# One pair in two of the second MLP product by seven block products, with two of their weight sums made by adding DMAs

## The chip, the cores and the metric

The kernel runs on one core of a Trainium2 chip. The metric is the time of one execution on the device, in microseconds (us). Engines and queues are named as the profile names them: PE (TensorE, matmuls), PEld (its weight loads), DVE (VectorE), ACT (ScalarE), POOL (GpSimd) and SP, whose queue issues the DMAs of the kernel before.

## What is computed

One layer of a bidirectional encoder on 256 tokens of width 2048, in float32: mixed attention, cross attention to 256 memory tokens, and an MLP of width 8192, each followed by a layer norm. The change touches the last of them:

```python
def squared_relu_mlp(h, w_mlp_in, w_mlp_out):
    return jnp.square(jax.nn.relu(h @ w_mlp_in)) @ w_mlp_out

ff = squared_relu_mlp(x, w_mlp_in[l], w_mlp_out[l])
x = layer_norm(ALPHA * x + ff, ln3_g[l], ln3_b[l])
```

## The kernel before

**Precision.** A float32 factor is split into a high part hi (a copy by ACT into the fast matmul type, L80) and a rest lo (a subtraction by DVE, L81). `mm3` (L145 to L148) multiplies two split factors by three matmuls: high by high, high by low, low by high. Four buffers for weights' hi and four for lo (`w_hi`, `w_lo`, 1024 columns each) pass the weights to TensorE.

**Stages of the MLP.** The 8192 hidden rows are worked off in four chunks (c) of 16 tiles of 128. In each chunk come four *hidden groups* (g) of four tiles: `hidden_group` multiplies the normed tokens `x2t` by eight double steps of `w_mi` (loaded 1 MB at a time into three buffers `raw`) and `hidden` squares the result (L726 to L728) and splits it into `ht`. Then come two *pair products* (q = 0 and 1, each 1024 output columns; the last chunk has q = 0 only and finishes with plain products from `w_ml`). So there are seven pair products.

**A pair product.** `pair_product(c, q)` takes the chunk's 16 row tiles of `w_mo` as eight pairs (p). A pair's unit is 1 MB: four blocks of 512 columns, in the order b12, b11, b22, b21. With the four blocks of `ht` it is a two by two block product. A *plain* pair takes eight block products of three matmuls, 24 matmuls of 512 columns, from two splits of 1024 columns. A pair listed in `SEVEN` takes seven block products, 21 matmuls, after Winograd's scheme; it needs four sums of weight blocks. `hidden` makes the sums of activations for such a pair (four small subtractions and additions, L743, and a split into `sums_h`) once per chunk. In the kernel before `SEVEN` holds pairs 2, 5 and 7. Their weight sums are made by DVE (L789): one instruction of 1024 columns (b11 + b12 and b22 + b12, with b12 broadcast) and two of 512 (the former's half + b22, and that + b21, each on the sum before it). Such a pair is split in four parts, of 1024, 512, 1024 and 1024 columns.

**Ends of a product.** Four results in `acc` are added to the residual rows `res` by DVE (L846 or L849, here called first adds), four in `att` are copied out by ACT (L857) and eight adds of 512 columns (L852) are left in a list `side`. `part` makes one split and then pops one weight sum from the list `sums`, or, if there is none, one piece of `side`.

**Loads.** `load_unit` issues the load of a unit two pairs ahead from SP. Units 0, 1, 4 and 5 use two fixed halves of a big tile `wx`, the others the three `raw` buffers. The other half of `wx` holds the two buffers of weight sums, used in turn. `wx` takes the place of the first half of hidden group 0's weights (`wide_0`), so nothing may be written there before TensorE has read these. During the hidden groups 1 and 2 of chunk 0 the residual's gain and bias rows (`ln2_g`, `ln2_b`, 256 KB each, broadcast to all partitions) come through `tmp` buffers, and DVE applies them (L566).

**Order.** A scheduler places each engine's instructions by its own estimate of the time; each engine then works them off strictly in that order, and each queue issues its DMAs in order.

Of the kernel before, what the change touches and what calls it, by code (L numbers as in the profile page):

```python
# [12 lines left out]
F32R = mybir.dt.float32r  # L13
BF16 = mybir.dt.bfloat16
AF = mybir.ActivationFunctionType
ALU = mybir.AluOpType
# [22 lines left out]
def encoder_kernel(ctx: ExitStack, tc: tile.TileContext, t, out):  # L39
# [672 lines left out]

    early.close()
    late = ctx.enter_context(tc.tile_pool(name="late", bufs=1))
    SEVEN = ((2, 5, 7), (2, 5, 7))
    s_in = Stream(t["w_mi"][4:])
    sts = [stats_tile() for _ in range(NB)]
    ht = big3("ht")
    sums_h = late.tile([P, 3072], F32R, name="sums_h").rearrange("p (u l c) -> p u l c", l=2, c=512)
    wx = big.tile([P, 8192], F32, tag="big", name="wx")  # L720
    raw2, sums_w = [[wx[:, o:o + 2048] for o in (i, i + 2048)] for i in (0, 4096)]

# [36 lines left out]
    def hidden_group(nexts, tiles, j0):  # L759
# [7 lines left out]
        for i in range(0, G, 2):  # L767
# [1 line left out]

    units = [(c, q, p) for c in range(NCH) for q in range(2) for p in range(CH // 2)  # L770
             if not (c == NCH - 1 and q == 1)]
    loaded, sums, slots = deque(), deque(), [0]

    def load_unit(chunk):

        if not units or units[0][0] != chunk:
            return
        c, q, p = units.pop(0)
        seven = p in SEVEN[q]
        raw = raw2[p % 4] if p % 4 < 2 else raw_tile()  # L780
        nc.sync.dma_start(raw, t["w_mo"][(c * 2 + q) * (CH // 2) + p])
        s = None
        if seven:
            s = sums_w[slots[0] % 2]
            slots[0] += 1
            b12, b22, b21 = [raw[:, o:o + 512] for o in (0, 1024, 1536)]

            def add(out, a, b):
                sums.append(lambda: nc.vector.tensor_tensor(out=out, in0=a, in1=b, op=ALU.add))  # L789
            add(s[:, 0:1024].rearrange("p (i c) -> p i c", i=2), raw[:, 512:1536].rearrange("p (i c) -> p i c", i=2),  # L790
                b12[:, None, :].broadcast_to([P, 2, 512]))
            add(s[:, 1024:1536], s[:, 0:512], b22)
            add(s[:, 1536:2048], s[:, 1024:1536], b21)
        loaded.append((raw, s))

    def part(src):
        w = src.shape[1]
# [9 lines left out]
    def pair_product(c, q):  # L807

        x11, x12, x21, x22 = [acc_tile() for _ in range(4)]
        p1, p5, p6, p7 = [att_tile() for _ in range(4)]  # L810
        plain = [p for p in range(CH // 2) if p not in SEVEN[q]]
        for p in range(CH // 2):
            load_unit(c)
            raw, s = loaded.popleft()
            k = 2 * p

            def a(k_, b):
                return ht[:, k_, b * P:(b + 1) * P], ht[:, k_, S + b * P:S + (b + 1) * P]

            def sm(i):  # L820
                u = SEVEN[0].index(p)
                return sums_h[:, u, 0, i * P:(i + 1) * P], sums_h[:, u, 1, i * P:(i + 1) * P]

            if p in SEVEN[q]:
                first, last = p == SEVEN[q][0], p == SEVEN[q][-1]
                while sums:
                    sums.popleft()()
                for src, todo in ((raw[:, 512:1536], ((p1, a(k, 0), first), (x12, sm(3), False))),
                                  (raw[:, 1536:2048], ((x11, a(k + 1, 0), False),)),
                                  (s[:, 0:1024], ((p5, sm(0), first), (p7, sm(2), first))),  # L830
                                  (s[:, 1024:2048], ((p6, sm(1), first), (x21, a(k + 1, 1), False)))):
                    for (hi, lo), (ps, (ah, al), start) in zip(part(src), todo):
                        mm3(ps, ah, al, hi, lo, start, last)
            else:
                for i in range(2):
                    w = part(raw[:, i * 1024:(i + 1) * 1024])
                    for (hi, lo), to in zip(w, ((x12, x22), (x11, x21))):
                        for b in range(2):
                            ah, al = a(k + i, b)
                            mm3(to[b], ah, al, hi, lo, p == 0 and i == 0, to[b] is x22 and p == plain[-1] and i == 1)  # L840
        cols = [slice((2 * q + i) * 512, (2 * q + i + 1) * 512) for i in range(2)]
        r11, r12, r21, r22 = [res[b][:, cc] for b in range(NB) for cc in cols]

        def first_add(r, ps):
            if c == 0:
                nc.vector.scalar_tensor_tensor(out=r, in0=r, scalar=ALPHA, in1=ps,  # L846
                                               op0=ALU.mult, op1=ALU.add)
            else:
                nc.vector.tensor_tensor(out=r, in0=r, in1=ps, op=ALU.add)  # L849

        def add(o, x, y, op=ALU.add):
            side.append(lambda: nc.vector.tensor_tensor(out=o, in0=x, in1=y, op=op))  # L852

        first_add(r22, x22)
        m1, m5, m7, m6 = [tmp_tile() for _ in range(4)]
        for m, ps in ((m1, p1), (m5, p5), (m7, p7), (m6, p6)):
            nc.scalar.activation(m, ps, AF.Copy)  # L857
        first_add(r12, x12)
        first_add(r11, x11)
        first_add(r21, x21)  # L860
        add(r22, r22, m5)
        add(r12, r12, m5)
        add(m6, m1, m6)
        add(m7, m6, m7)
        add(r11, r11, m1)
        add(r12, r12, m6, ALU.subtract)
        add(r21, r21, m7)
        add(r22, r22, m7, ALU.subtract)
        if c == NCH - 1:
            for b, r in ((0, r11), (0, r12), (1, r21), (1, r22)):  # L870
                side.append(lambda b=b, r=r: stats(sts[b], r))

    for c in range(NCH):
        for g in range(CH // G):
            first = c == 0 and g == 0
            if g == CH // G - 1:
                load_unit(c)
                load_unit(c)
            hidden_group((lambda k: w_mi0[k // 2]) if first else (lambda k: s_in.next()),
                         att_tile if g % 2 else acc_tile, g * G)  # L880
            if first:
                side.extend(residual("ln2"))
        for q in range(2):
            if c < NCH - 1 or q == 0:
                pair_product(c, q)
                continue
            s_ml = Stream(t["w_ml"])
            for n in (2, 3):
                if n == 3:
                    pump(len(side))  # L890
                    wide_w = [big.tile([P, 8192], F32R, tag="big", name=f"w{i}") for i in range(2)] + [None]
                    ps = proj_tokens(None, ht, CH, 512, by_block=True, wide=last_weights, tiles=att_tile)
                else:
                    ps = proj_tokens(s_ml, ht, CH, 512, by_block=False, tiles=acc_tile)
                for b, o, w, p_ in ps:
                    r = res[b][:, n * 512 + o:n * 512 + o + w]
                    nc.vector.tensor_tensor(out=r, in0=r, in1=p_[:, :w], op=ALU.add)
                    stats(sts[b], r)
# [139 lines left out]
```

## Time and profile before

| | |
|---|---|
| runs of the kernel before | 1108.9, 1110.0, 1110.2 us (median 1110.02) |
| profiled execution | 1109.3 us, of it 1107.5 us span |
| granted TensorE clock, mean | 0.996 |
| chunk 0: hidden groups 0 to 3 | about 402 to 493 us |
| chunk 0: products q = 0, q = 1 | 492.9 to 534.4, 534.4 to 575.9 us |
| bytes moved, mean | 215.86 MB, 195 GB/s |

A row of a timeline gives its start, its length, engine, line, operation, output and inputs with their shapes, how many instructions are merged and, in square brackets, how long the engine had been idle before and what ended this. A row of windows gives, for one stretch of time, the busy time of each engine with its count of instructions, the granted clock, the mean busy share of the sixteen DMA engines, and the rate. Successive instructions of one engine overlap by some 0.09 us in DVE's rows, so the step from start to start is shorter than one row's length. Starts are in microseconds from the start of the span.

### The profile page before, as it was taken

To read this page: it belongs to the slowest core of one execution; us is meant where nothing else is said; L and a number is where in the kernel's file an instruction comes from. 1 tells how busy PE (TensorE), PEld (TensorE's weight loads), DVE (VectorE), ACT (ScalarE), POOL (GpSimd) and SP (SyncE) were. 2 spreads that over 40 slices of the span, in tenths; PEclk is the share of its full clock that TensorE was granted. 3 is DMA by queue.
4 is the path that set the end of the run, shared out by engine and by line. 5 is a ranking of instruction groups with operands and counts; after the bars stand their busy time and mean duration, and the time that the engine had idled before them with its cause. 6 is when DMAs were issued, how large, how long until landed. Compare 5 with 4: busy or idle time off the path is not lost.

```text
span 1107.5 us, 15288 instructions
## 1 busy us (share of the span) xinstructions
PE 1091.5 (99%) x5941; PEld 942.8 (85%) x5941; DVE 858.3 (77%) x1257; ACT 587.2 (53%) x860; POOL 38.3 (3%) x45
## 2 busy tenths in 40 slices
PE   9999999999999999999999999999999999999996
PEld 6988899988999878888888888888888888888885
DVE  6878677688879687888977678978678887677796
ACT  6555566545576444455555445555445555555550
POOL 1402000000100000000000000000000000000000
PEclk9999999999999999999999999999999999999998
DMA  9664453466567427744566555455544556555372
GB/s 332 232 229 141 154 195 128 173 220 246 180 205 271 146 78 267 256 165 184 191 225 214 186 183 214 178 206 190 197 184 171 209 197 224 188 190 191 114 260 82
DMA packets 37944, 215.86 MB, mean 195 GB/s; under 512 B 4336, under 2 KB 5232, under 8 KB 14192
## 3 DMA queue, kind: packets, MB, share of 16 engines
q1 hardware_dynamic: 37872, 214.89, 54.4%
q8 instruction: 46, 0.75, 0.3%
q14 instruction: 26, 0.21, 0.1%
HBM read 212.78 MB, written 2.10 MB: 194 GB/s over the span
## 4 chain that ended last, share of the span: by engine, by line
PE 96%; DMA 2%; DVE 1%; SPq 0%; ACT 0%; issue 0%; POOL 0%; DVEq 0%; ACTq 0%
PE acc L147 15%; PE acc L146 15%; PE acc L148 15%; PE acc L195 11%; PE att L195 11%; PE att L200 5%; PE acc L200 5%; PE att L148 3%; PE att L147 3%; PE att L146 3%; PE acc L188 2%; PE acc L186 2%; PE acc L187 2%; PE att L535 1%; PE att L350 1%; DMA raw<-in_w_ka 1%
## 5 line engine op out<-in xcount | busy, mean ns | idle before, releaser
L81 DVE TENSOR_TENSOR w_lo<-raw,w_hi 128x1024 fp32r<-128x1024 f32 (+2 forms) x318 | 365.3, 1162 | 129.6 <-ACT w_hi L80 127.3
L80 ACT ACTIVATE w_hi<-raw 128x1024 fp32r<-128x1024 f32 (+2 forms) x318 | 318.0, 1011 | 275.6 <-PE acc L148 103.0
L80 ACT ACTIVATE w_hi<-wx 128x1024 fp32r<-128x1024 f32 x98 | 100.8, 1031 | 119.5 <-PE acc L148 85.5
L81 DVE TENSOR_TENSOR w_lo<-wx,w_hi 128x1024 fp32r<-128x1024 f32 x98 | 115.0, 1185 | 53.9 <-ACT w_hi L80 53.9
L195 PE MATMUL att<-x2t,w_hi 128*128 128x512 f32 x512 | 139.6, 394 | 0.0
L147 PE MATMUL acc<-w_lo,ht 128*128 128x512 f32 x354 | 137.8, 389 | 0.0
L148 PE MATMUL acc<-w_hi,ht 128*128 128x512 f32 x354 | 137.7, 389 | 0.0
L195 PE MATMUL acc<-x2t,w_hi 128*128 128x512 f32 x480 | 132.3, 394 | 0.0
L146 PE MATMUL acc<-w_hi,ht 128*128 128x512 f32 x354 | 111.4, 389 | 0.0
L195 PEld LDWEIGHTS att<-x2t,w_hi 128*128 128x128 f32 x512 | 88.1, 189 | 12.3
L195 PEld LDWEIGHTS acc<-x2t,w_hi 128*128 128x128 f32 x480 | 82.6, 189 | 11.5
L200 PEld LDWEIGHTS att<-x2t,w_lo 128*128 128x128 f32 x512 | 77.5, 189 | 10.2
L200 PEld LDWEIGHTS acc<-x2t,w_lo 128*128 128x128 f32 x480 | 73.3, 189 | 9.5
L200 PE MATMUL att<-x2t,w_lo 128*128 128x256 f32 x512 | 80.2, 281 | 0.0
L147 PEld LDWEIGHTS acc<-w_lo,ht 128*128 128x128 f32 x354 | 66.5, 188 | 14.0 <-DVE w_lo L81 0.2
L146 PEld LDWEIGHTS acc<-w_hi,ht 128*128 128x128 f32 x354 | 66.4, 188 | 13.8
L148 PEld LDWEIGHTS acc<-w_hi,ht 128*128 128x128 f32 x354 | 66.4, 188 | 13.8
L200 PE MATMUL acc<-x2t,w_lo 128*128 128x256 f32 x480 | 77.0, 281 | 0.0
L147 PE MATMUL acc<-w_lo,xt 128*128 128x512 f32 (+2 forms) x192 | 69.4, 363 | 0.6 <-DVE w_lo L81 0.6
L148 PE MATMUL acc<-w_hi,xt 128*128 128x512 f32 (+2 forms) x192 | 69.1, 361 | 0.0
L146 PE MATMUL acc<-w_hi,xt 128*128 128x512 f32 (+2 forms) x192 | 65.6, 361 | 1.0 <-ACT w_hi L80 1.0
L148 PE MATMUL acc<-w_hi,ot 128*128 128x512 f32 (+1 forms) x136 | 51.9, 382 | 0.0
(244 smaller groups left out, 1876.7 us busy)
## 6 DMA issues: line engine op xcount, KB each, us to landing
raw<-in_w_mi SPq DMA_DIRECT2D x64, 1024.0 KB, 4.9
wx<-in_w_mo SPq DMA_DIRECT2D x28, 1024.0 KB, 4.8
raw<-in_w_mo SPq DMA_DIRECT2D x28, 1024.0 KB, 4.8
raw<-in_w_out SPq DMA_DIRECT2D x16, 1024.0 KB, 4.9
raw<-in_w_ml SPq DMA_DIRECT2D x8, 1024.0 KB, 5.0
raw<-in_w_b SPq DMA_DIRECT2D x5, 1024.0 KB, 4.8
raw<-in_w_qa SPq DMA_DIRECT2D x16, 256.0 KB, 5.4
raw<-in_w_qa SPq DMA_DIRECT2D x4, 1024.0 KB, 4.9
```

Source lines behind the costliest of these rows:

```text
L80: pin(nc.scalar.activation(hi, src, AF.Copy), pinned)
L81: return pin(nc.vector.tensor_tensor(out=lo, in0=src, in1=f(hi), op=ALU.subtract), pinned)
L146: nc.tensor.matmul(ps, ah, bh, start=start, stop=False)
L147: nc.tensor.matmul(ps, ah, bl, start=False, stop=False)
L148: nc.tensor.matmul(ps, al, bh, start=False, stop=stop)
L186: nc.tensor.matmul(ps, hi, xt[:, k, 0:S], start=k == 0, stop=False)
L187: nc.tensor.matmul(ps, hi, xt[:, k, S:2 * S], start=False, stop=False)
L188: nc.tensor.matmul(ps, lo, xt[:, k, 0:S], start=False, stop=k == nk - 1)
L195: nc.tensor.matmul(ps, hi[:, i * P:(i + 1) * P], xt[:, k, :], start=k == 0, stop=k == nk - 1)
L200: nc.tensor.matmul(ps[:, 0:S], lo[:, i * P:(i + 1) * P], xt[:, k, 0:S], start=False, stop=False)
L350: nc.tensor.transpose(pp[:, st * S + b * P:st * S + b * P + P], ev[:, b, st * P:(st + 1) * P], ident)
L535: nc.tensor.transpose(ps[:, o:o + P], x(b, k // 4)[:, (k % 4 + j) * P:(k % 4 + j + 1) * P], ident)
```

## The change

`SEVEN` becomes pairs 1, 3, 5 and 7, in both q. Of the four weight sums of such a pair two are now made in memory: `load_halves` has SP load block b12 twice, side by side, into a buffer of 1024 columns, and then has POOL issue a DMA that adds the blocks b11 and b22 (1024 columns) onto it. Three such buffers stand in the former sums' place and are refilled in turn: the first three in chunk 0 ahead of hidden groups 1 to 3, each later one when a pair has been used. DVE makes the other two sums (512 columns each) in a single buffer `t24`. A unit of such a pair is loaded without its first 512 columns.

```diff
-    SEVEN = ((2, 5, 7), (2, 5, 7))
+    SEVEN = ((1, 3, 5, 7), (1, 3, 5, 7))
...
-    sums_h = late.tile([P, 3072], F32R, name="sums_h").rearrange("p (u l c) -> p u l c", l=2, c=512)
+    sums_h = late.tile([P, 4096], F32R, name="sums_h").rearrange("p (u l c) -> p u l c", l=2, c=512)
...
-    loaded, sums, slots = deque(), deque(), [0]
+    loaded, sums, halves = deque(), deque(), deque()
+    sevens = deque(u for u in units if u[2] in SEVEN[u[1]])
+    t24 = sums_w[0][:, 0:1024]
+    spare = deque([sums_w[0][:, 1024:2048], sums_w[1][:, 0:1024], sums_w[1][:, 1024:2048]])
+
+    def load_halves():
+
+        if not sevens:
+            return
+        c, q, p = sevens.popleft()
+        s, src = spare[0], t["w_mo"][(c * 2 + q) * (CH // 2) + p]
+        spare.rotate(-1)
+        nc.sync.dma_start(s.rearrange("p (i c) -> p i c", i=2),
+                          src[:, 0:512][:, None, :].broadcast_to([P, 2, 512]))
+        nc.gpsimd.dma_start(s, src[:, 512:1536], accum_op=ALU.add)
+        halves.append(s)
...
-        nc.sync.dma_start(raw, t["w_mo"][(c * 2 + q) * (CH // 2) + p])
-        s = None
+        o = 512 if seven else 0
+        nc.sync.dma_start(raw[:, o:], t["w_mo"][(c * 2 + q) * (CH // 2) + p][:, o:])
+        s, todo = None, []
         if seven:
-            s = sums_w[slots[0] % 2]
-            slots[0] += 1
-            b12, b22, b21 = [raw[:, o:o + 512] for o in (0, 1024, 1536)]
-
-            def add(out, a, b):
-                sums.append(lambda: nc.vector.tensor_tensor(out=out, in0=a, in1=b, op=ALU.add))
-            add(s[:, 0:1024].rearrange("p (i c) -> p i c", i=2), raw[:, 512:1536].rearrange("p (i c) -> p i c", i=2),
-                b12[:, None, :].broadcast_to([P, 2, 512]))
-            add(s[:, 1024:1536], s[:, 0:512], b22)
-            add(s[:, 1536:2048], s[:, 1024:1536], b21)
-        loaded.append((raw, s))
+            s = halves.popleft(), t24
+            b22, b21 = raw[:, 1024:1536], raw[:, 1536:2048]
+            for o, a, b in ((t24[:, 0:512], s[0][:, 0:512], b22), (t24[:, 512:1024], t24[:, 0:512], b21)):
+                todo.append(lambda o=o, a=a, b=b: nc.vector.tensor_tensor(out=o, in0=a, in1=b, op=ALU.add))
+        loaded.append((raw, s, todo))
...
-            raw, s = loaded.popleft()
+            raw, s, _ = loaded.popleft()
+            if loaded:
+                sums.extend(loaded[0][2])
...
-                                  (s[:, 0:1024], ((p5, sm(0), first), (p7, sm(2), first))),
-                                  (s[:, 1024:2048], ((p6, sm(1), first), (x21, a(k + 1, 1), False)))):
+                                  (s[0], ((p5, sm(0), first), (p7, sm(2), first))),
+                                  (s[1], ((p6, sm(1), first), (x21, a(k + 1, 1), False)))):
...
+                load_halves()
...
+            if c == 0 and 0 < g:
+                load_halves()
```

In the changed kernel the lines behind these move: the weight sums of DVE are L803 (before: L789), the first adds L859 and L862 (L846 and L849), the epilogue's adds L865 (L852), the broadcast loads L784, the adding DMAs L786 and the unit loads L797 (L781).

**The turn from q = 0 to q = 1 in chunk 0, on DVE.** In the program before these rows stand behind the last split of q = 0. `w_lo_5363` and `w_lo_5380` belong to pair 0, `w_lo_5399` and `w_lo_5416` to pair 1, which is plain.

```order
L846 SCALAR_TENSOR_TENSOR res0_1487<-res0_1487,acc_5041 128x512
L846 SCALAR_TENSOR_TENSOR res0_1487<-res0_1487,acc_5040 128x512
L81 TENSOR_TENSOR w_lo_5363<-wx_4240,w_hi_5362 128x1024
L81 TENSOR_TENSOR w_lo_5380<-wx_4240,w_hi_5379 128x1024
L852 TENSOR_TENSOR res0_1487<-res0_1487,tmp_5341 128x512
L852 TENSOR_TENSOR res1_1488<-res1_1488,tmp_5342 128x512
L852 TENSOR_TENSOR res0_1487<-res0_1487,tmp_5342 128x512
L846 SCALAR_TENSOR_TENSOR res1_1488<-res1_1488,acc_5042 128x512
L81 TENSOR_TENSOR w_lo_5399<-wx_4240,w_hi_5398 128x1024
L852 TENSOR_TENSOR tmp_5344<-tmp_5341,tmp_5344 128x512
L81 TENSOR_TENSOR w_lo_5416<-wx_4240,w_hi_5415 128x1024
L852 TENSOR_TENSOR tmp_5343<-tmp_5344,tmp_5343 128x512
```

In the changed program the same place reads as follows; `w_lo_5424` is the first part of pair 1, which is now one of seven products.

```order
L859 SCALAR_TENSOR_TENSOR res0_1487<-res0_1487,acc_5054 128x512
L859 SCALAR_TENSOR_TENSOR res0_1487<-res0_1487,acc_5053 128x512
L803 TENSOR_TENSOR wx_4240<-wx_4240 128x512
L81 TENSOR_TENSOR w_lo_5388<-wx_4240,w_hi_5387 128x1024
L81 TENSOR_TENSOR w_lo_5405<-wx_4240,w_hi_5404 128x1024
L865 TENSOR_TENSOR res0_1487<-res0_1487,tmp_5366 128x512
L865 TENSOR_TENSOR res1_1488<-res1_1488,tmp_5367 128x512
L865 TENSOR_TENSOR res0_1487<-res0_1487,tmp_5367 128x512
L803 TENSOR_TENSOR wx_4240<-wx_4240 128x512
L859 SCALAR_TENSOR_TENSOR res1_1488<-res1_1488,acc_5055 128x512
L81 TENSOR_TENSOR w_lo_5424<-wx_4240,w_hi_5423 128x1024
L865 TENSOR_TENSOR tmp_5369<-tmp_5366,tmp_5369 128x512
```

Directly behind it, still on DVE in the changed program, come pair 1's other three parts (`w_lo_5435`, `w_lo_5443`, `w_lo_5454`) and the first part of pair 2 (`w_lo_5468`):

```order
L81 TENSOR_TENSOR w_lo_5435<-wx_4240,w_hi_5434 128x512
L865 TENSOR_TENSOR tmp_5368<-tmp_5369,tmp_5368 128x512
L865 TENSOR_TENSOR res0_1487<-res0_1487,tmp_5369 128x512
L81 TENSOR_TENSOR w_lo_5443<-wx_4240,w_hi_5442 128x1024
L865 TENSOR_TENSOR res1_1488<-res1_1488,tmp_5368 128x512
L81 TENSOR_TENSOR w_lo_5454<-wx_4240,w_hi_5453 128x1024
L865 TENSOR_TENSOR res1_1488<-res1_1488,tmp_5368 128x512
L81 TENSOR_TENSOR w_lo_5468<-raw_5385,w_hi_5467 128x1024
```

Two weight sums (L803) have moved into this place, and four parts of a pair of seven stand between the adds where two parts of a plain pair stood. In TensorE's order of the changed product (its first matmul counted 0) `w_lo_5443` is first used by matmul 40, `w_lo_5454` by matmul 44, `w_lo_5468` by matmul 50 and the second part of pair 2, `w_lo_5485`, by matmul 62; these are the rows of PE from matmul 37 to matmul 44:

```order
L146 MATMUL acc_5378<-w_hi_5467,ht_4238 128x512
L146 MATMUL acc_5380<-w_hi_5467,ht_4238 128x512
L146 MATMUL acc_5377<-w_hi_5467,ht_4238 128x512
L147 MATMUL att_5382<-w_lo_5443,sums_h_4239 128x512
L148 MATMUL att_5382<-w_hi_5442,sums_h_4239 128x512
L147 MATMUL att_5384<-w_lo_5443,sums_h_4239 128x512
L148 MATMUL att_5384<-w_hi_5442,sums_h_4239 128x512
L147 MATMUL att_5383<-w_lo_5454,sums_h_4239 128x512
```

High products of pair 2 (`w_hi_5467`) stand ahead of the products that need pair 1's lo parts.

**Chunk 0, hidden groups 1 and 2, on SP.** Before, behind the sixth load of `w_mi` (`raw_4541`):

```order
L134 DMA raw_4541<-in_w_mi 128x2048
L562 DMA tmp_4407<-in_ln2_g 128x512
L562 DMA tmp_4409<-in_ln2_b 128x512
L562 DMA tmp_4499<-in_ln2_g 128x512
L781 DMA wx_4240<-in_w_mo 128x2048 x2
L134 DMA raw_4620<-in_w_mi 128x2048
L562 DMA tmp_4501<-in_ln2_b 128x512
```

And now, behind the same load (`raw_4550`), where POOL's adding DMAs each wait for one of the three broadcasts:

```order
L134 DMA raw_4550<-in_w_mi 128x2048
L784 DMA wx_4240<-in_w_mo 128x2x512 x3
L797 DMA wx_4240<-in_w_mo 128x2048
L797 DMA wx_4240<-in_w_mo 128x1536
L134 DMA raw_4631<-in_w_mi 128x2048
L562 DMA tmp_4416<-in_ln2_g 128x512
L562 DMA tmp_4418<-in_ln2_b 128x512
L562 DMA tmp_4508<-in_ln2_g 128x512
L562 DMA tmp_4510<-in_ln2_b 128x512
```

The residual's rows have moved behind the broadcasts, two units and one more load of `w_mi`. On DVE the changed program has, ahead of hidden group 2's first split (`w_lo_4634`) and its third (`w_lo_4682`, shown in the second piece), the adds that need these rows:

```order
L566 TENSOR_TENSOR res0_1487<-res0_1487,tmp_4416 128x512
L566 TENSOR_TENSOR res1_1488<-res1_1488,tmp_4416 128x512
L81 TENSOR_TENSOR w_lo_4634<-raw_4631,w_hi_4633 128x1024
L81 TENSOR_TENSOR w_lo_4659<-raw_4631,w_hi_4658 128x1024
L803 TENSOR_TENSOR wx_4240<-wx_4240 128x512
L566 TENSOR_TENSOR res0_1487<-res0_1487,tmp_4418 128x512
L566 TENSOR_TENSOR res1_1488<-res1_1488,tmp_4418 128x512
L566 TENSOR_TENSOR res0_1487<-res0_1487,tmp_4508 128x512
L566 TENSOR_TENSOR res1_1488<-res1_1488,tmp_4508 128x512
L803 TENSOR_TENSOR wx_4240<-wx_4240 128x512
```

Behind them, without a gap in the listing:

```order
L727 TENSOR_TENSOR tmp_4594<-att_4406,tmp_4594 128x256
L727 TENSOR_TENSOR tmp_4600<-att_4407,tmp_4600 128x256
L727 TENSOR_TENSOR tmp_4606<-att_4408,tmp_4606 128x256
L566 TENSOR_TENSOR res0_1487<-res0_1487,tmp_4510 128x512
L727 TENSOR_TENSOR tmp_4612<-att_4409,tmp_4612 128x256
L566 TENSOR_TENSOR res1_1488<-res1_1488,tmp_4510 128x512
L728 SCALAR_TENSOR_TENSOR tmp_4594<-tmp_4594 128x256
L728 SCALAR_TENSOR_TENSOR tmp_4600<-tmp_4600 128x256
L728 SCALAR_TENSOR_TENSOR tmp_4606<-tmp_4606 128x256
L728 SCALAR_TENSOR_TENSOR tmp_4612<-tmp_4612 128x256
L81 TENSOR_TENSOR w_lo_4682<-raw_4679,w_hi_4681 128x1024
```

Before, the residual's adds stood ahead of these places in ones and twos, and no weight sum stood among them.

## Prediction, made before the result was known

> **What bounds the kernel now.** I began with the page's busy line and its chain of work, then asked who waits for whom on TensorE.
>
> ```profile
> PE 1091.5 (99%) x5941; PEld 942.8 (85%) x5941; DVE 858.3 (77%) x1257; ACT 587.2 (53%) x860; POOL 38.3 (3%) x45
> PE 96%; DMA 2%; DVE 1%; SPq 0%; ACT 0%; issue 0%; POOL 0%; DVEq 0%; ACTq 0%
> PE acc L146 <- ACT w_hi L80: 1.0, 2, 0.7
> PE acc L147 <- DVE w_lo L81: 0.6, 1, 0.6
> ```
>
> TensorE is busy nearly all the time and is 96% of the chain. All it ever waits for weights is 1.6 us. So a matmul less is time less, and any wait of TensorE is time more, one for one. Nothing else moves the end. Next I read one pair product (chunk 0, q = 1) in the timeline of TensorE and its window:
>
> ```profile
> 534.42 0.84 PE L146 MATMUL acc<-w_hi,ht 128*128 128x512 f32 x3
> 535.10 0.39 PE L147 MATMUL acc<-w_lo,ht 128*128 128x512 f32 x1
> ...
> 575.90 0.84 PE L195 MATMUL acc<-x2t,w_hi 128*128 128x512 f32 x3
> core 0: us, PE busy (x) PEld busy (x) DVE busy (x) ACT busy (x) POOL busy (x), PEclk, DMA share, GB/s
> 534.42:575.90 41.48, 41.48 (x185) 34.35 (x183) 35.72 (x41) 23.01 (x28) 0.00 (x0) 1.00 0.55 203
> ```
>
> The product begins at 534.42 and the next hidden group at 575.90. Five plain pairs of 24 matmuls and three pairs of 21 are 183 matmuls in 41.48 us: 0.2267 us each, at full granted clock. VectorE is busy for 35.72 of these 41.48 us, so what it does and **when** matters.
>
> **What is removed from TensorE.** Each product changes one plain pair into one of seven block products: 183 matmuls become 180, and seven products lose 21. 21 x 0.2267 = **-4.8 us**. No matmul is added.
>
> **What VectorE gains and loses.** Per product the three wide weight sums go (3 x 1024 columns). Two more sums of 512 columns come (8 for 6). The splits become 12 of 1024 and four of 512 in the pairs of seven, and eight of 1024 in the plain ones: 20 and 4, where 19 and 3 stood. Back to back, 1024 columns take 1.13 us (538.19 to 539.32 below) and 512 take 0.60 (537.59 to 538.19). -3.4 + 1.2 + 1.1 + 0.6 = -0.5 us per product: VectorE is hardly relieved. The new weight sums of activations (four small adds and a split per chunk) fall into the first hidden group of a chunk, where TensorE's rate leaves VectorE idle; I cost them at nothing. If that cover failed they would cost 1.5 us in each of four chunks.
>
> **Where VectorE's order now hurts: the turn from q = 0 to q = 1.** The old rows there:
>
> ```profile
> 532.32 1.28 DVE L846 SCALAR_TENSOR_TENSOR res<-res,acc 128x512 f32<-128x512 f32 x2
> 533.51 2.35 DVE L81 TENSOR_TENSOR w_lo<-wx,w_hi 128x1024 fp32r<-128x1024 f32 x2
> 535.78 1.89 DVE L852 TENSOR_TENSOR res<-res,tmp 128x512 f32<-128x512 f32 x3
> 537.59 0.68 DVE L846 SCALAR_TENSOR_TENSOR res<-res,acc 128x512 f32<-128x512 f32 x1
> 538.19 1.22 DVE L81 TENSOR_TENSOR w_lo<-wx,w_hi 128x1024 fp32r<-128x1024 f32 x1
> 539.32 0.69 DVE L852 TENSOR_TENSOR tmp<-tmp 128x512 f32<-128x512 f32 x1
> ```
>
> VectorE runs without a gap from 532.32 on, 2.10 us before TensorE starts the product (call that E = 534.42). The first w_lo is ready at 534.73 and used at 535.10: 0.4 us to spare. In the new order (shown in the section on the change) this place gets two more sums, and pair 1, which asks for four parts within 21 matmuls, takes the place of a plain pair that asked for two within 24. From E - 2.10 the new order runs: two first adds 1.20, a sum 0.60, two splits 2.26, three adds 1.80, a sum 0.60, an add 0.60, split 1.13, add 0.60, split of 512 0.60, two adds 1.20, split 1.13, add 0.60, split 1.13, add 0.60, split 1.13. The last of them (pair 2, first part) ends at E - 2.10 + 15.18 + 0.09 (the tail of a single row) = E + 13.2. TensorE's order first uses it after 50 matmuls, at E + 11.3. Likewise pair 1's third part: ready E + 9.7, wanted after 40 matmuls, E + 9.1. The second part of pair 2 is wanted after 62, E + 14.1 plus the delay, and is ready at E + 14.3. So TensorE loses about 13.2 - 11.3 = 1.8 us and then catches up with nothing. The same order stands in chunks 0, 1 and 2 (the last chunk has no second product): 3 x 1.8 = **+5.5 us**. Bounds: the steps add errors of some 0.06 us a piece over 16, so 0.8 to 2.8 each, 2.5 to 8.4 in all.
>
> **What the queues get: chunk 0, hidden groups 1 and 2.** SP's queue now holds three broadcast loads and both first weight units ahead of the residual's rows (its order is in the section on the change).
>
> ```profile
> 371.62 50.84 SPq L134 DMA_DIRECT2D raw<-in_w_mi  x6
> 422.50 0.43 SPq L562 DMA_DIRECT2D tmp<-in_ln_g  x1
> ...
> 429.12 0.33 SPq L134 DMA_DIRECT2D raw<-in_w_mi  x1
> 429.79 0.33 SPq L562 DMA_DIRECT2D tmp<-in_ln_b  x1
> ...
> 439.84 1.29 DVE L566 TENSOR_TENSOR res<-res,tmp 128x512 f32<-128x512 f32 x2 [0.50 <-DMA tmp<-in_ln_b]
> ...
> 428.00:434.00 6.00, 6.00 (x37) 5.29 (x36) 5.68 (x10) 3.04 (x6) 0.00 (x0) 1.00 1.01 325
> 434.00:440.00 6.00, 6.00 (x36) 5.25 (x35) 5.50 (x9) 2.56 (x3) 0.00 (x0) 1.00 0.98 378
> 440.00:446.00 6.00, 6.00 (x36) 5.20 (x35) 3.49 (x4) 2.35 (x3) 0.00 (x0) 1.00 0.92 306
> ```
>
> The sixth w_mi load goes out at 422.5, and from 428 to 446 the sixteen engines are 92 to 101% busy: here, unlike in the products (0.55), transfers have no room. Between 422.5 and the landing of the second ln_b row at 439.84 there came 1 + 0.75 + 2 + 1 + 0.25 = 5.0 MB (page's KB), 3.5 us a MB. The new queue brings, up to the first ln_g row, 1 + 1.5 + 1.75 + 1 + 0.25 = 5.5 MB, and beside it three accumulating loads of 0.5 MB on POOL's queue. No row of before shows such a load. Without any share of theirs the row lands at 422.5 + 19.1 = 441.6. With them at the price of a plain load 7.0 MB, 446.7; at twice that 451.8. The nearest row is that of the plain loads of the same tensor:
>
> ```profile
> wx<-in_w_mo SPq DMA_DIRECT2D x28, 1024.0 KB, 4.8
> ```
>
> An accumulation writes the same bytes from the same tensor, and it waits only for a broadcast that stands early in the queue; so I take the plain load's price, 446.7, and keep both ends for the range.
>
> The Trainium skill, "DMA: Bandwidth & Descriptors", section "Issuing engines are not separate DMA queues", says that loads issued from GpSimd run on the same sixteen engines and interleave with SP's. By that rule the term below is 4.3 us; if POOL's loads ran on lanes of their own it would be 0. No run here has a load from POOL yet.
>
> VectorE now has that row's add ahead of the splits of hidden group 2 and, behind it, work in this order up to group 2's third split (w_lo_4682): two adds, two splits, a sum (it waits for the first accumulation), four adds, a sum, three additions of the hidden group just ended (L727), an add, a fourth L727, an add, four squares (L728), the split. L727 and L728, of 256 columns, step by 0.34:
>
> ```profile
> 471.08 0.42 DVE L728 SCALAR_TENSOR_TENSOR tmp<-tmp 128x256 f32<-128x256 f32 x1
> 471.42 0.75 DVE L727 TENSOR_TENSOR tmp<-acc,tmp 128x256 f32<-128x256 f32 x2
> ...
> 454.57 0.64 PE L200 MATMUL acc<-x2t,w_lo 128*128 128x256 f32 x4
> ```
>
> That is 10 x 0.60 + 3 x 1.13 + 8 x 0.34 + 0.09 = 12.2 us. TensorE, unchanged up to there, wants this split at 454.57. 446.7 + 12.2 - 454.6 = **+4.3 us**; with the two bounds 0 (it would be 0.8 early) and 9.4.
>
> Costed at nothing: POOL's wait for each broadcast (POOL has no other work between the norms), SP's later broadcasts, each of which waits for the split of the buffer it refills (behind it stand units wanted four or more pairs later), and the extra bytes in the products: 8.4 MB become 11.5 in 40.8 us, a share of about 0.55 x 1.39 = 0.77. If an accumulation cost several loads this cover is gone (rival 3).
>
> **The sum.** -4.8 + 5.5 + 4.3 = +5.0 us on the profiled execution, 1109.3 us (span 1107.5): 1114.3. It lies 0.7 below the median of the runs shown; on the median of 1110.0 the forecast is 1115.0.
>
> **Rivals.** (1) The turns cost as worked out but the start of chunk 0 is covered (accumulations land late or use gaps, so the rows land by 442): -4.8 + 5.5 = +0.7, 1110.7. For it: the low bound above is 0. Against: the windows at 0.92 to 1.01. (2) Both are covered: VectorE finishes a little sooner than my steps, TensorE's order, which brings later parts' w_hi products forward, hides the rest: -4.8, **1105.2**, faster. It decides at once if the split of pair 2 is ready by E + 11.3. For it: VectorE's total per product falls by 0.5 us and TensorE has waited for it 0.6 us in all so far. Against: four parts in pair 1 directly behind the epilogue's adds. (3) The accumulating loads cost several plain loads. Loads then pass one whole product's time from about (1 - 0.48 - 0.14) / 0.14 = 2.7 times a plain load's price per byte (0.48 is the share of the plain units left, 0.14 that of the broadcasts, 0.14 that of the accumulations at plain price). At 4 times the share is 1.18 and seven products lose 7 us each: some 1160. Against: nothing here, only that no row shows such a price. (4) That the change does not do what it says: it takes sums off VectorE, but puts as much back in splits. It is part of the forecast already.
>
> **Chances.** Forecast (both delays, 1111 to 1121) 0.53; rival 1 0.22; rival 2 0.16; rival 3 0.09. A measurement of this kernel tells about 0.2% (2.2 us) from no change. Faster by more: rival 2 less its upper edge, 0.14. Within 0.2%: rival 1 and the lower edge of the forecast, 0.29. Slower: 0.57. The range reaches from 1105 (rival 2) to 1121 (the forecast with the upper bound of one of its delays); rival 3 and the far tails lie outside, some 0.15. The forecast's own range is 1111 to 1121.
>
> **What would show it.** The waits of TensorE: if I am right, it waits for VectorE's w_lo some 1.8 us just behind each of three turns from q = 0 to q = 1, and some 4 us at the third split of chunk 0's hidden group 2; VectorE's add of the first ln_g row waits for its DMA until about 447. TensorE should show 21 matmuls less. The forecast is wrong if TensorE shows no wait there (rival 2), if the ln rows land by 442 (rival 1), or if the DMA share in the products stands at 1 (rival 3).

## The result, and the profile after

The changed kernel takes 1120.9 us (median of four runs, 1118.8 to 1121.0); the kernel before took 1109.8 beside it (1108.9 to 1110.2). The ratio is 1.009, with a 95% interval of 1.0078 to 1.0102: slower, by 11 us where the forecast had 5. The profiled execution has a span of 1119.1 us against 1107.5, so 11.6 us are to be found.

First the page of the changed kernel, its busy line and its chain of work, and what TensorE waited for in its matmuls and in its weight loads:

```profile
PE 1095.4 (98%) x5920; PEld 939.5 (84%) x5920; DVE 861.4 (77%) x1284; ACT 597.2 (53%) x878; POOL 62.9 (6%) x73
PE 85%; DVE 8%; DMA 4%; ACT 1%; issue 1%; SPq 0%; DVEq 0%; POOL 0%; ACTq 0%
PE acc L200 <- DVE w_lo L81: 5.1, 5, 2.5
PE att L147 <- DVE w_lo L81: 1.5, 3, 0.5
PE acc L147 <- DVE w_lo L81: 1.3, 4, 0.8
PEld acc L200 <- DVE w_lo L81: 7.2, 5, 2.9
PEld acc L147 <- DVE w_lo L81: 5.8, 11, 1.0
```

TensorE runs 21 matmuls less and yet is busy 3.9 us more: "busy" also counts the time that a matmul takes at a lower clock, and part of TensorE's waits (in q = 1 below 42.05 us at a clock of 1.00, for the 180 matmuls that take 40.81 in q = 0). VectorE and DMAs, 3% of the chain before, are 12% now. The waits do not add up to the loss, since short ones lie in the weight loads and behind modelled ends of matmuls. So the lengths of stages are the better measure. The windows of before and of after, cut where TensorE starts chunk 0's hidden groups, its product q = 0, its product q = 1 and the next chunk's hidden groups:

```profile
402.41:492.93 90.52, 90.52 (x520) 79.22 (x519) 70.02 (x108) 45.78 (x68) 0.00 (x0) 1.00 0.63 219
492.93:534.42 41.49, 41.49 (x185) 34.35 (x183) 35.86 (x49) 24.40 (x33) 0.00 (x0) 1.00 0.49 183
575.90:665.64 89.74, 89.74 (x514) 78.50 (x512) 63.59 (x94) 44.21 (x63) 0.00 (x0) 1.00 0.57 196
```

```profile
402.66:501.85 99.19, 94.23 (x520) 81.48 (x519) 70.25 (x112) 45.66 (x69) 2.80 (x3) 0.97 0.67 226
501.85:542.66 40.81, 40.81 (x182) 33.80 (x181) 34.20 (x49) 25.59 (x34) 2.59 (x3) 1.00 0.77 233
542.66:585.56 42.90, 42.05 (x181) 33.34 (x180) 37.75 (x45) 24.45 (x29) 3.47 (x4) 1.00 0.93 272
585.56:675.76 90.20, 90.02 (x514) 78.41 (x513) 64.07 (x97) 44.70 (x64) 0.87 (x1) 1.00 0.61 209
```

The product q = 0 takes 40.81 us, 180 x 0.2267: the gain is there, in full. Everything else is loss: +8.7 us at the start of chunk 0, +2.1 in q = 1 (42.90 - 40.81), and +0.45 in the next hidden groups. The last two come again in each of chunks 0, 1 and 2 (q = 0 and 1 together 83.71, 83.73, 83.72; hidden groups behind them 90.20, 90.19, 90.15). So -4.8 + 8.7 + 3 x 2.1 + 3 x 0.45 = 11.55, nearly all of the 11.6.

**The start of chunk 0.** VectorE and TensorE in the timeline there, and the granted clock in windows of 2 us:

```profile
449.66 1.29 DVE L566 TENSOR_TENSOR res<-res,tmp 128x512 f32<-128x512 f32 x2 [10.49 <-DMA tmp<-in_ln_g]
...
460.62 1.22 DVE L81 TENSOR_TENSOR w_lo<-raw,w_hi 128x1024 fp32r<-128x1024 f32 x1
```

```profile
452.14 1.23 PE L200 MATMUL acc<-x2t,w_lo 128*128 128x256 f32 x4 [2.05 <-DVE w_lo L81]
...
461.89 1.05 PE L200 MATMUL acc<-x2t,w_lo 128*128 128x256 f32 x4 [2.48 <-DVE w_lo L81]
```

```profile
452.00:454.00 2.00, 1.86 (x6) 1.69 (x7) 2.00 (x4) 0.00 (x0) 0.00 (x0) 0.50 1.00 418
454.00:456.00 2.00, 2.00 (x10) 1.70 (x9) 2.00 (x4) 1.83 (x2) 0.00 (x0) 0.68 0.90 279
456.00:458.00 2.00, 2.00 (x13) 1.75 (x12) 2.00 (x6) 0.18 (x1) 0.00 (x0) 1.00 0.95 357
...
462.00:464.00 2.00, 2.00 (x7) 1.74 (x8) 2.00 (x6) 1.04 (x2) 0.00 (x0) 0.53 0.02 8
464.00:466.00 2.00, 2.00 (x9) 1.80 (x8) 2.00 (x6) 1.06 (x1) 0.00 (x0) 0.62 0.71 209
```

VectorE stands still for 10.5 us, until 449.66, when the first ln_g row is there; the third split of hidden group 2 is done at 461.84, 12.2 us behind the row. TensorE gets to its matmuls at 461.89 instead of 454.57. This is the forecast's mechanism, step by step, with the row 3 us later. TensorE also waits at the group's first split (452.14), where the forecast named no wait. And behind each of TensorE's two gaps its clock falls to about half for some 3.5 us (7 matmuls in two microseconds, where a full-speed window has 13).

**The turn from q = 0 to q = 1.** The changed kernel's product q = 1 begins at E = 542.66. VectorE's rows for the last part of pair 1 and the first of pair 2, and TensorE's weight loads that wait for them:

```profile
552.96 1.21 DVE L81 TENSOR_TENSOR w_lo<-wx,w_hi 128x1024 fp32r<-128x1024 f32 x1
554.10 0.68 DVE L865 TENSOR_TENSOR res<-res,tmp 128x512 f32<-128x512 f32 x1
554.70 2.35 DVE L81 TENSOR_TENSOR w_lo<-raw,w_hi 128x1024 fp32r<-128x1024 f32 x2
```

```profile
554.23 0.19 PEld L147 LDWEIGHTS att<-w_lo,sums_h 128*128 128x128 f32 x1 [0.95 <-DVE w_lo L81]
555.96 0.19 PEld L147 LDWEIGHTS acc<-w_lo,ht 128*128 128x128 f32 x1 [0.51 <-DVE w_lo L81]
```

Pair 1's last part is ready at 554.17, and pair 2's first split (the first of the two in the third row) at about 555.9. That is E + 13.3, where the forecast's steps gave E + 13.2. TensorE takes each as soon as it is there.

### The profile page after: what moved, and what is told of

It is laid out like the page before. It is cut to its first block, busy times and chain, and to the rows that moved or that the text cites. A ratio compares the mean times of both kernels' runs of the same rounds, so it can differ in the third digit from the quotient of the medians.

```text
span 1119.1 us, 15454 instructions
## 1 busy us (share of the span) xinstructions
PE 1095.4 (98%) x5920; PEld 939.5 (84%) x5920; DVE 861.4 (77%) x1284; ACT 597.2 (53%) x878; POOL 62.9 (6%) x73
## 3 DMA queue, kind: packets, MB, share of 16 engines
q0 software_dynamic: 4032, 14.68, 7.5%
## 4 chain that ended last, share of the span: by engine, by line
PE 85%; DVE 8%; DMA 4%; ACT 1%; issue 1%; SPq 0%; DVEq 0%; POOL 0%; ACTq 0%
PE acc L147 12%; PE acc L148 12%; PE acc L146 12%; PE acc L195 10%; PE att L195 9%; PE acc L200 5%; PE att L200 5%; DVE w_lo L81 4%; PE att L148 3%; PE att L147 3%; PE att L146 3%; PE acc L188 2%; PE acc L186 2%; PE acc L187 2%; DMA tmp<-in_ln_g 2%; ACT w_hi L80 1%
## 5 line engine op out<-in xcount | busy, mean ns | idle before, releaser
L80 ACT ACTIVATE w_hi<-wx 128x1024 fp32r<-128x1024 f32 x112 | 110.7, 1006 | 121.3 <-PE acc L148 87.5
L81 DVE TENSOR_TENSOR w_lo<-wx,w_hi 128x1024 fp32r<-128x1024 f32 x112 | 128.4, 1154 | 58.6 <-ACT w_hi L80 57.9
L147 PE MATMUL acc<-w_lo,ht 128*128 128x512 f32 x312 | 122.2, 392 | 0.8 <-DVE w_lo L81 0.5
L148 PE MATMUL acc<-w_hi,ht 128*128 128x512 f32 x312 | 121.5, 389 | 0.0
L146 PE MATMUL acc<-w_hi,ht 128*128 128x512 f32 x312 | 98.2, 391 | 0.3
L147 PEld LDWEIGHTS acc<-w_lo,ht 128*128 128x128 f32 x312 | 58.6, 188 | 15.5 <-DVE w_lo L81 3.6
L146 PEld LDWEIGHTS acc<-w_hi,ht 128*128 128x128 f32 x312 | 58.3, 188 | 13.9 <-ACT w_hi L80 1.5
L148 PEld LDWEIGHTS acc<-w_hi,ht 128*128 128x128 f32 x312 | 58.6, 188 | 12.1
L786 POOL DMA_DIRECT2D wx<-in_w_mo x28 | 24.6, 878 | 613.6 <-DVE wx L803 200.7
```

The costliest lines, as they stand in the source:

```text
L80: pin(nc.scalar.activation(hi, src, AF.Copy), pinned)
L81: return pin(nc.vector.tensor_tensor(out=lo, in0=src, in1=f(hi), op=ALU.subtract), pinned)
L146: nc.tensor.matmul(ps, ah, bh, start=start, stop=False)
L147: nc.tensor.matmul(ps, ah, bl, start=False, stop=False)
L148: nc.tensor.matmul(ps, al, bh, start=False, stop=stop)
L786: nc.gpsimd.dma_start(s, src[:, 512:1536], accum_op=ALU.add)
```

## The experiments

Theory A: the loss is made at three places, each by something that stands ahead of the work that TensorE needs next: loads ahead of the residual's rows on SP's queue, epilogue additions ahead of pair 1's splits, and (not in the forecast) a weight sum ahead of a turn's first split. The rivals are named with the runs. All ratios are to the kernel before, run beside each.

### The two places, apart and together

Run `late` puts the first three broadcasts behind the last row of the residual:

```diff
-            if c == 0 and 0 < g:
-                load_halves()
             if g == CH // G - 1:
+                for _ in range(3 if c == 0 else 0):
+                    load_halves()
...
-        nc.sync.dma_start(s.rearrange("p (i c) -> p i c", i=2),
-                          src[:, 0:512][:, None, :].broadcast_to([P, 2, 512]))
+        tc.add_manual_dep(nc.sync.dma_start(s.rearrange("p (i c) -> p i c", i=2),
+                                            src[:, 0:512][:, None, :].broadcast_to([P, 2, 512])).ins,
+                          rows_at[-1].ins.name, mybir.DependencyInfo(
+                              mybir.DependencyClass.NoSync, mybir.DependencyReason.DATA))
```

> The first three broadcasts, and with them the first three accumulating loads, are put behind the last of the residual's ln_b rows on SP's queue; all else is as in the change. Theory A (the start of chunk 0 loses 8.9 us because the residual's rows queue behind these loads): TensorE's waits at 452 and 461 go, chunk 0's four hidden groups take 90.5 us as before instead of 99.2, and the time is 1120.9 - 8.9 = 1112.0. Rival B (the accumulating loads slow the weight loads wherever they stand): the delay moves to hidden groups 3 and 4, and the time stays above 1117.

Run `hold` ties q = 0's additions to a later split of VectorE:

```diff
+            held[0] = q == 1 and p < 2
...
-        split(hi[:, :w], lo[:, :w], src)
+        behind[0] = split(hi[:, :w], lo[:, :w], src)
...
-        else:
+        elif not held[0]:
             pump()
...
+                if q == 0:
+                    tc.add_manual_dep(ins.ins, behind[0].ins.name, mybir.DependencyInfo(
+                        mybir.DependencyClass.NoSync, mybir.DependencyReason.DATA))
```

> The eight epilogue additions of q = 0 are held back on VectorE until the second split of the plain pair 2 of q = 1 and then go one by one; start of chunk 0 as in the change. Theory A (each turn loses 2.1 us because the additions stand ahead of pair 1's splits): a wait of some 0.35 us per turn stays, where one sum and two first additions stand ahead of the first split; the rest goes, 3 x 1.75 = 5.2 us, and the time is 1115.7. Rival C (at the turn TensorE waits for VectorE's total work or for loads, not for the order of the additions): the same loss appears a few pairs later, and the time stays within 1 us of 1120.9.

Run `both` has the two edits together.

> Both edits together. Theory A, if the two losses are independent: 1120.9 - 8.9 - 5.2 = 1106.8, faster than before by 3 us (0.3%). Rivals B and C: 1112 or more.

Run `all` also ties the additions of q = 1 to splits of the next hidden group (`if c < NCH - 1` in place of `if q == 0`, and `behind[0]` set by the stream of `w_mi` too).

> As both, and the additions of q = 1 are also held, each behind one split of the next chunk's first hidden group. In the changed kernel the hidden groups of chunks 1 to 3 take 0.44 us more than before each. Theory A (the same cause, additions ahead of the first splits): another 1.3 us less, 1105.5. If that loss comes from elsewhere (loads, the first additions): as both, 1106.8.

| run | time, us | ratio, 95% interval | chunk 0's groups | q = 0 and 1 of chunk 0 | groups of chunk 1 |
|---|---|---|---|---|---|
| changed kernel | 1120.9 | 1.009 (1.0078 to 1.0102) | 99.19 | 83.71 | 90.20 |
| late | 1112.0 | 1.0019 (1.0009 to 1.0028) | 90.51 | 83.71 | 90.15 |
| hold | 1115.1 | 1.0042 (1.0027 to 1.0057) | 96.88 | 82.08 | 90.22 |
| both | 1107.3 | 0.9971 (0.9959 to 0.9982) | 90.52 | 82.09 | 90.20 |
| all | 1107.1 | 0.9972 (0.9962 to 0.9982) | 90.67 | 82.09 | 90.18 |

`late` takes the start's loss away and leaves the products as they were, so rival B falls. `hold` takes 1.6 of the 2.1 us of each turn (in its trace the additions begin behind the first split of pair 3, one split later than expected); its start is shorter than the change's too, though nothing was edited there: the row came 1 us earlier (448.66), and the clock fell behind the first gap only (below). Together they are faster than before. `all` missed: holding q = 1's additions gave nothing, and the hidden groups still took 0.44 us too long. So the additions were not the cause there. VectorE's rows in `all` at that turn (TensorE starts the hidden group at 575.48):

```profile
573.43 1.28 DVE L864 SCALAR_TENSOR_TENSOR res<-res,acc 128x512 f32<-128x512 f32 x2
574.62 0.69 DVE L807 TENSOR_TENSOR wx<-wx 128x512 f32<-128x512 f32 x1
575.22 2.35 DVE L81 TENSOR_TENSOR w_lo<-raw,w_hi 128x1024 fp32r<-128x1024 f32 x2
577.49 1.29 DVE L871 TENSOR_TENSOR res<-res,tmp 128x512 f32<-128x512 f32 x2
```

Two first additions, then a weight sum (L807) of a pair that TensorE reaches only 90 us later, in the next chunk, and then the split that it needs at once. Why the scheduler put the sum there was not tested; that its inputs were there at that time is a guess.

### The sum at the turns

Run `sums_held` is `all` with each of VectorE's weight sums tied to the split at which the code calls it:

```diff
-                todo.append(lambda o=o, a=a, b=b: nc.vector.tensor_tensor(out=o, in0=a, in1=b, op=ALU.add))
+                todo.append(lambda o=o, a=a, b=b: tc.add_manual_dep(
+                    nc.vector.tensor_tensor(out=o, in0=a, in1=b, op=ALU.add).ins, behind[0].ins.name,
+                    mybir.DependencyInfo(mybir.DependencyClass.NoSync, mybir.DependencyReason.DATA)))
```

> As all, and each of VectorE's two sums of a pair of seven is also held behind the split at which the code calls it. Order in all: at both turns (q = 0 to 1, and q = 1 to the next chunk) a sum for a later pair stands between two first additions and the first split, and TensorE waits 0.18 us there by the waits, 0.35 and 0.44 us by the length of the stages. Theory A (that sum is the cause): both go, 3 x 0.79 = 2.4 us less than all, 1104.8; that is before less the 21 matmuls (1105.0). Rival D (the two first additions alone are the cause, or the loads): as all, 1107.1.

1104.05 us, ratio 0.9946 (0.9934 to 0.9959): faster than before by 5.6 us, and than the changed kernel by some 16. Its windows, cut as above:

```profile
402.14:492.65 90.51, 90.51 (x521) 79.21 (x520) 70.34 (x112) 46.08 (x69) 2.85 (x3) 1.00 0.74 247
492.65:533.46 40.81, 40.81 (x182) 33.79 (x181) 34.23 (x48) 25.59 (x35) 2.60 (x3) 1.00 0.76 231
533.46:574.25 40.79, 40.79 (x181) 33.78 (x180) 37.55 (x45) 24.65 (x29) 3.46 (x4) 1.00 0.96 289
574.25:663.99 89.74, 89.74 (x513) 78.50 (x512) 64.21 (x98) 44.67 (x64) 0.87 (x1) 1.00 0.61 209
```

TensorE is busy all through each of these stages, in both products. VectorE does the same work in q = 1 as in the changed kernel (37.55 us against 37.75): only its order is another. The DMA engines are 96% busy in q = 1, and neither TensorE, VectorE nor ScalarE waits for a DMA there.

### What an accumulating load costs

In run `plain_pool` POOL's load has no `accum_op`: the same bytes come, but b12 is not added. In run `no_acc` POOL's load is left out altogether.

> The accumulating loads on GpSimd's queue become plain loads of the same bytes from the same queue; left out is the addition of b12. In the change the first ln_g row reaches VectorE at 449.66 (448.66 in hold, the same up to there), 3 us later than the 446.7 of the forecast, which priced an accumulation as a plain load. Theory P (the accumulation itself costs about 1.6 plain loads): now it lands near 446.7, the third split's delay falls from 7.1 to about 4.3 us, and the time is 1118, or 1116.5 if the granted clock also stays up. Rival Q (the price is that of GpSimd's queue, or of the broadcasts): the row still comes at 448.7 to 449.7 and the time stays at 1120 to 1121.

> The loads on GpSimd's queue are left out (and with them the addition of b12 and b22 to b12); the broadcasts stay where they are. The forecast's lower end for this case: the first ln_g row at 441.6, no wait at the third split, chunk 0's groups at 90.5 to 91 us, time 1112. Rival Q2 (the broadcast loads, which repeat 512 columns, are dearer than their bytes): the row at 444 or later, and some of the delay stays.

VectorE's first row of the residual in the two, and the queue of POOL's loads in the changed kernel and in `plain_pool` (packets, MB, share of the sixteen engines' span):

```profile
445.39 1.29 DVE L566 TENSOR_TENSOR res<-res,tmp 128x512 f32<-128x512 f32 x2 [6.25 <-DMA tmp<-in_ln_g]
```

```profile
442.40 1.29 DVE L566 TENSOR_TENSOR res<-res,tmp 128x512 f32<-128x512 f32 x2 [1.44 <-DMA tmp<-in_ln_g]
```

```profile
q0 software_dynamic: 4032, 14.68, 7.5%
```

```profile
q0 software_dynamic: 4032, 14.68, 4.0%
```

| run | row at | chunk 0's groups | time, us |
|---|---|---|---|
| no_acc | 442.40 | 90.54 | 1112.5 (ratio 1.0023, 1.0014 to 1.0033) |
| plain_pool | 445.39 | 93.46 | 1115.7 (1.0051, 1.0038 to 1.0065) |
| changed kernel, second profile | 448.77 | 97.32 | 1119.6 (1.0085, 1.0068 to 1.0102) |
| changed kernel, first profile | 449.66 | 99.19 | 1120.9 (1.009, 1.0078 to 1.0102) |

The executions do not reach this place at the same time, so the row is best counted from the issue of the sixth `w_mi` load, at 422.84 in `no_acc`, 422.36 in `plain_pool`, 421.86 and 422.38 in the changed kernel's second and first profile: 19.6, 23.0, 26.9 and 27.3 us. (In `hold` it is 26.5.) Three plain loads of 0.5 MB thus delay the row by 3.5 us, three accumulating ones by 6.9 to 7.7: about twice as much. The queue says the same, 7.5% against 4.0% for the same bytes. So the accumulation itself has the price, not GpSimd's queue (rival Q). The broadcasts cost about their bytes: without POOL's loads the row comes 19.6 us behind that load, where the forecast's lower end has 19.5 (441.6, with the load at 422.13 in the profile before). So rival Q2, dearer broadcasts, falls. By the row's time the delay follows the forecast's formula: 445.39 + 12.2 - 454.6 = 3.0, and the groups took 93.46 - 90.52 = 2.9 us more.

This also bears on the page of the Trainium skill that the prediction cites, "DMA: Bandwidth & Descriptors", section "Issuing engines are not separate DMA queues": loads started by GpSimd pushed SP's row back by 3.5 us even when plain, which agrees with it.

### The clock behind the gaps

Run `after_again` is the changed kernel once more. In run `warm` TensorE multiplies by zero in the two gaps, adding nothing to the results:

```diff
+        if dummies and part is his:
+            for i in range(dummies):
+                nc.tensor.matmul(outs[i % 4], zeros, ones[:, None, :].broadcast_to([P, 4, P]), start=False, stop=False)
...
+                         {0: 7, 4: 9} if c == 0 and g == 2 else {})
```

> The change itself, for a second profile beside warm. In the first profile the granted clock fell to 0.50 for some 3.5 us after each of two gaps of TensorE (452 and 462), in hold, the same up to there, only once. Theory G (the drop follows a gap of 2 to 3 us, but not every one): time 1120 to 1121; the number of drops in the profile may be 0, 1 or 2, and chunk 0's hidden groups take 97.5 us with none behind the second gap, 99.2 with one.

> The change with 16 matmuls by zero (128x512, adding nothing) that TensorE runs inside the two gaps: 7 (1.6 us) ahead of the first w_lo matmuls of chunk 0's hidden group 2, 9 (2.0 us) ahead of those of its third double step. Theory G (the clock fell because TensorE stood still): granted clock 1.00 throughout, chunk 0's groups 97.4 us (the row's lateness alone: 449.7 + 12.2 - 454.6 = 7.2 above 90.5 is 97.7), 1.5 us less than after_again. If the clock falls for another cause (power at that point, DMA): it falls as before and the time is that of after_again.

`after_again`: 1119.6 us (ratio above); in its profile the clock fell behind the first gap alone, and the groups took 97.32 us. `warm`: 1119.4 us, ratio 1.0082 (1.0067 to 1.0097), groups 97.62. TensorE in `warm`, and its clock behind the gap:

```profile
457.46 2.12 PE L209 MATMUL acc<-ones,zeros 128*128 128x512 bf16 x9
461.51 0.74 PE L202 MATMUL acc<-x2t,w_lo 128*128 128x256 f32 x4 [1.93 <-DVE w_lo L81]
```

```profile
462.00:464.00 2.00, 2.00 (x14) 1.73 (x13) 2.00 (x5) 1.45 (x2) 0.00 (x0) 1.00 0.05 8
```

The zeros do not fill the gaps: idle stretches of 0.51 and 1.93 us are left. With them TensorE keeps the full clock in every window from 444 to 472. That fits a gap as the cause but does not show it: it is one execution, `after_again` kept its clock through a gap of 2.33 us, and `plain_pool` through one of 2.68. And the time was that of `after_again`, not 1.5 us less: a fall behind the first gap is hidden, since TensorE waits at the third split anyway, and the second had not happened there. What the second costs can be read by taking off the third split's lateness (its end less the time at which TensorE wants it, 52.16 us behind the start of the groups). In `hold`, `after_again`, `warm` and `plain_pool` the groups lose 0.13 to 0.17 us more than that lateness; in the first profile, with the second fall, they lose 8.67 for a lateness of 7.02, 1.65 more. So that fall cost some 1.5 us.

### Are the adding loads needed?

Run `dve_sums` is the kernel before with `SEVEN` and `sums_h` of the change and all sums on VectorE. Run `dve_held` is that with the additions and sums tied as in `sums_held`.

> The kernel before with pairs 1, 3, 5 and 7 by seven products and all sums on VectorE, so without the adding loads. VectorE's steps in a q = 1 product: 4 x 1.13 wide sums, 8 x 0.60, 20 x 1.13 and 4 x 0.60 splits, 12 x 0.60 additions: 41.5 us, above TensorE's 40.8. Theory A: no loss at the start of chunk 0 (90.5 us), but the turns lose more than the 2.1 us of the change, by the wide sum of 1.13 that pair 1 adds there, or two: 3.2 to 4.4 each; 1109.8 - 4.8 + 3 x 3.2 to 4.4 + 1.3 = 1116 to 1119. Rival E (VectorE has room for these sums): as late, 1112.

> dve_sums with the same holding of additions and sums as in sums_held: seven products in pairs 1, 3, 5 and 7, no adding loads, VectorE's order repaired. Theory A (taking two sums off VectorE by DMA is needed): VectorE's 41.5 us in a q = 1 product are more than TensorE's 40.8, and TensorE loses 1 to 2.5 us in each: 1108 to 1112. Rival F (the order alone decides, the adding loads bring nothing): 1104 to 1105.5, as sums_held.

`dve_sums`: 1114.8 us, ratio 1.0042 (1.0028 to 1.0055), below the 1116 to 1119 expected, but nearer to it than to the rival's 1112. Its start is free (90.49), its products of chunks 0 to 2 take 84.47, 86.47 and 84.45, against 81.6 in `sums_held`. `dve_held`: 1108.2 us, ratio 0.9982 (0.9973 to 0.9991). Its windows of q = 0 and q = 1:

```profile
493.04:533.90 40.86, 40.86 (x182) 33.85 (x181) 38.53 (x53) 25.67 (x35) 0.00 (x0) 1.00 0.51 187
533.90:575.78 41.88, 41.19 (x182) 33.59 (x180) 39.65 (x46) 24.36 (x30) 0.00 (x0) 1.00 0.58 201
```

With its order repaired VectorE still costs TensorE 1.1 us in each q = 1. So the adding loads are worth 4.1 us (1108.2 less 1104.05) once the order is right, of which 3 x 1.1 lie here; most of what the changed kernel lost was order, not load.

## Why the prediction was right, and where it was too small

The direction and the two places were right. The size was not: the kernel lost 11.1 us where the sum had 5.0, and 1120.9 lies only 0.1 us inside the stated range of 1105 to 1121. That it lies inside is partly luck.

- **TensorE, -4.8:** right. 40.81 us a product, as computed.
- **VectorE's total, -0.5 us per product:** right. Over the whole program its weight sums take 54.5 us before and 38.2 after, its splits of the units in `wx` 115.2 and 128.4: -3.1 us, -0.44 per product. The windows of chunk 0's products (71.95 us against 71.58) do not show it, since instructions of the neighbouring stages fall into them. The conclusion drawn from it (hardly relieved) held.
- **The turns, 3 x 1.8:** right in place and cause, 2.1 us each, inside the bounds of 0.8 to 2.8. `hold` shows that the additions make 1.6 of it; the rest went with `sums_held`, as a sum ahead of the first split. The two do not simply add in the order: TensorE loses the worst lateness along the way, and when that goes, the next worst appears.
- **The start of chunk 0, +4.3:** right in mechanism, mis-sized: 8.7. The row came at 449.7 instead of 446.7, because an accumulating load was priced as a plain one; `plain_pool` and `no_acc` show that it costs twice that. The price of a plain load was too high as well: three took 3.5 us, where the sum had 5.1. So the bound "at twice that 451.8" was 2.1 us too late, as the value taken was 3.0 too early. The chain of 12.2 us behind the row was exact. The clock behind the second gap, some 1.5 us in one profile and nothing in the other, was no term at all.
- **The turns from q = 1 to the next chunk: missing from the sum.** They lose 0.45 us three times, by a sum that the scheduler put ahead of the first split; `sums_held` takes it away.
- **The rivals.** Rival 3 was right that an accumulation costs more than a plain load, but the price is about two, below the 2.7 from which it saw the loads pass a product's time. The product q = 0 ran at a DMA share of 0.77, as forecast, and q = 1 at 0.93 (0.96 in `sums_held`), and TensorE did not wait for a DMA there. Rivals 1 and 2 fall with the waits shown.

The forecast's sum was +5.0, the profile's is +11.6. The later row (3.0), the clock (1.5) and the two kinds of turn (3 x 0.3 and 3 x 0.45) make 6.75 and account for the 6.6 that lacked within 0.2 us.

## What to carry to other kernels

When a product gets shorter, look at what stands ahead of the first split that TensorE needs behind each turn: three orders, none of them more work, turned a gain of 5.6 us into a loss of 11. Queue loads that are wanted in 60 us behind small loads that are wanted now. And price a DMA that adds at two plain loads, as measured here for loads of 0.5 MB in float32.

## What the runs showed of the hardware

An accumulating load of 0.5 MB takes about twice the DMA engines' time of a plain one (7.5% against 4.0% of the span for 14.68 MB).

TensorE's clock can fall to half behind a short gap. The gaps that TensorE's waits list at this place were 2.05 and 2.48 us in the first profile (both followed by a fall), 1.99 and 2.35 in `hold` and 2.38 and 2.33 in `after_again` (the first followed by one, the second not), 2.68 in `plain_pool` and 1.93 in `warm` (none). So the length of the gap alone does not decide. The Trainium skill, "TensorE: Matmul & The Clock Gate", section "What's actually happening", says that activity is judged in windows of about 3.4 us that run on freely, and that the clock is halved after an idle one. The half rate (0.50) agrees with these rows, and windows that run on freely would fit that the length does not decide, which no run here tests. The idle window does not agree: gaps of 1.99 to 2.48 us, shorter than such a window, were already followed by a fall, and there the measurement decides.
